# Moving the two parts of the normed input to a pool of their own, at the front of the on-chip memory

## The chip, the cores and the metric

The kernel runs on one core of a Trainium2 chip. The metric is the device time of one execution in microseconds (us); of several runs the median is given.

## The reference, cut to what matters

One layer of a model with four parallel mixers. The input `x` (512 rows of 1024) is normed and multiplied by one wide weight matrix; the columns of the product are the inputs of the four mixers and the gates:

```
h = rms_norm(x, norm_g)                      # 512 x 1024
proj = h @ w_in                              # 1024 x 11208, split into 19 parts
y_a = chunked_spatial_gating(a_u, a_v, ...) * silu(a_z)
y_b = dsa_attention(b_q, b_c, ...)          * silu(b_z)   # top 128 keys of each query
y_c = short_gated_conv(c_b, c_c, c_x, ...)  * silu(c_z)
y_d = forgetting_attention(d_q, d_k, d_v, d_f, ...) * silu(d_z)
branch = einsum('nbsw,nwd->bsnd', [y_a, y_b, y_c, y_d], w_branch)
merged = sum(sigmoid(gates) * branch, axis=n)
out = rms_norm(x + merged @ w_out, final_g)
```

## The kernel before, in words

**Numbers in two parts.** All large products run in float32r on TensorE. To keep float32's precision each operand is split into a high part (rounded to float32r by ScalarE) and a low part (the rest, a subtraction on VectorE or GpSimd); a product is then the sum of three matmuls, high by high, high by low, low by high. The helper is `split` (lines 73 to 81; its instructions appear as L76, L77, L79 and L80).

**The normed input** lies on chip in its two parts, `hh` and `hl`, from start to end. Each has 128 partitions of 8 x 512 float32r numbers (16,384 bytes in each partition): feature within a block of 128 along the partitions, then the block `k` (0 to 7), then the 512 rows of `x`. They are written once, by `transposed_x` (L230 to L237), and read by every product with `w_in`:

- `proj_fm` (L110 to L121) is called 80 times. Each call makes 24 matmuls into one PSUM tile `ps_fm`: the weights `wh`, `wl` are the stationary operand (128 x 128), and a whole row block of `hh` or `hl` is the moving operand (512 columns).
- `term_tm` (L139 to L142) makes three matmuls with the input as the stationary operand and 512 columns of weights moving. It is used with `hh`, `hl` for `ps_dv` (L246 to L250, 96 matmuls) and for `ps_va` (L594 to L598, 96 matmuls), and with the merged branches `mh`, `ml` for `ps_o` at the end (L791 to L795).

```
114	        for k in range(NK):
115	            nc.tensor.matmul(ps[:m], wh[:, k, :], hh[:, k, :], start=(k == 0), stop=False)
116	            nc.tensor.matmul(ps[:m], wh[:, k, :], hl[:, k, :], start=False, stop=False)
...
119	        for k in range(NK):
120	            nc.tensor.matmul(ps[:m], wl[:, k, :], hh[:, k, :], start=False, stop=(k == NK - 1))
...
140	        nc.tensor.matmul(ps, ah, wh, start=(k == 0), stop=False)
```

(The first argument is the output, the second the stationary, the third the moving operand.)

**Order of the work.** First the input is normed and transposed, with the products for the attention's values between (`ps_dv`). Then come the small projections of the sparse attention and its scores (`dots`, L456 and L457), the values of the first mixer (`ps_va`), and the search for the top 128 keys: 16 rounds of max and match-replace on VectorE (L471 and L472), handed out step by step between projections by `point()`. Both attentions run in the same way between projections (`lg` logits, `pt_ps` transposes, `po` values). From about 303 us on, four pairs of `gated` (L716) and `merge` (L733) follow: a merge computes a gate by `proj_fm`, and after each gate the branch product `pb` of the one before (L742, L743 and L745, 12 matmuls each, with `yh`, `yl` moving). In each merge the last branch product follows directly on the one before it. Last comes the output product `ps_o`. Instructions are placed by a scheduler that keeps each engine's order fixed in the finished program.

**Where tiles lie.** A pool's tiles are laid one behind the other in the order of their allocation, each rounded up to 32 bytes in a partition, and pools are laid in the order in which they are opened: `const`, `wpool`, `sb`. In the program the first pool begins at byte 16,512 of each partition (258 x 64). `const` begins with these:

```
ident  512 bytes   at 16512  (258 x 64)
negh    32         at 17024  (266 x 64)
causal 512         at 17056  (266 x 64 + 32)
up    2048         at 17568  (274 x 64 + 32)
hh   16384         at 19616  (306 x 64 + 32)
hl   16384         at 36000  (562 x 64 + 32)
bfB     16         at 52384  (818 x 64 + 32)
prm    180         at 52416  (819 x 64), and from here on multiples of 64
```

All tiles of `wpool` (weights and raw weights) and all larger tiles of `sb` (among them `yh`, `yl`, `mh`, `ml`) begin at multiples of 64 bytes, and so do the slices of them that the 128 x 128 and 512-column operands named above read.

Of the kernel before, what the change touches and what calls it, by code (L numbers as in the profile page):

```python
# [9 lines left out]
F32R = mybir.dt.float32r  # L10
# [7 lines left out]
P = 128  # L18
S = 512
# [3 lines left out]
NK = D // P  # L23
# [10 lines left out]
def hybrid_kernel(ctx: ExitStack, tc, x, norm_g, w_in, gm_ln_g, gm_ln_b, gm_w_s, gm_b_s,  # L34
# [2 lines left out]
    x, w_in, out = x[0], w_in[0], out[0]  # L37
    PSUM = bass.MemoryType.PSUM

    const = ctx.enter_context(tc.tile_pool(name="const", bufs=1))  # L40
    wpool = ctx.enter_context(tc.tile_pool(name="wpool", bufs=1))
    sb = ctx.enter_context(tc.tile_pool(name="sb", bufs=1))
# [168 lines left out]
                            pattern=[[1, S]], channel_multiplier=-1)  # L211
    nc.vector.tensor_copy(up, upf)

    hh = const.tile([P, NK, S], F32R, name="hh")
    hl = const.tile([P, NK, S], F32R, name="hl")

    def norm_x(t):
        xt = xts[t // 2][:, t % 2, :]
# [649 lines left out]
```

## Time and profile before

| | |
|---|---|
| median of 3 runs | 718.44 us (717.96 to 719.29) |
| profiled execution, its own time | 719.16 us |
| span in its profile | 717.5 us, granted TensorE clock 0.999 |
| TensorE matmuls | 3139, busy 703.9 us of the span |
| VectorE, ScalarE, GpSimd busy | 361.3, 276.1, 170.6 us |

The span is the time from the first to the last instruction on the core; the rest of an execution's own time, 1.7 us here, lies around it. Matmuls are pipelined: the duration given for one reaches past the start of the next. So the pace of TensorE is read not from durations but from the distance between the starts of successive matmuls. In a timeline, successive instructions of one kind are merged into a row ("x8"), whose start is that of the first. In the view by stretches, an instruction that runs over a border is counted on both sides.

### The profile page before, as it was taken

What the parts mean: (1) busy time and instruction counts of PE and PEld (TensorE: products, weight loads), DVE (VectorE), ACT (ScalarE), POOL (GpSimd) and SP (SyncE); (2) the same over time, 40 slices, a digit from 0 to 9 for tenths busy, and PEclk for the clock granted to TensorE, in tenths of its full rate; (3) what the DMA queues carried; (4) which work ended last, traced back from release to release, by engine and by line L of the source; (5) the groups of instructions that cost most, each with busy time, mean ns of one, the idle gap of its engine ahead of it and who ended that gap; (6) DMA issues with size and microseconds to landing.
All of it is one profiled execution on the core that took longest, in us unless ns stands there. A gap on an engine that the chain in (4) does not pass through costs nothing.

```text
span 717.5 us, 8000 instructions
## 1 busy us (share of the span) xinstructions
PE 703.9 (98%) x3139; PEld 564.8 (79%) x3139; DVE 361.3 (50%) x638; ACT 276.1 (38%) x439; POOL 170.6 (24%) x110
## 2 busy tenths in 40 slices
PE   7999999998999999999999999999999999999996
PEld 4878767787888888888888888888888888888885
DVE  5725699999763755534222442233422334333454
ACT  4616354345545656333232232222322223333232
POOL 1000487342232422112000121113211131111101
PEclk9999999999999999999999999999999999999999
DMA  6715031322121122223133131331313313133133
GB/s 235 220 60 153 3 117 59 103 75 60 58 89 59 60 63 94 79 88 118 60 117 112 64 118 60 117 118 58 118 59 117 118 58 118 59 117 118 59 118 117
DMA packets 56817, 68.05 MB, mean 95 GB/s; under 512 B 3582, under 2 KB 45067, under 8 KB 56780
## 3 DMA queue, kind: packets, MB, share of 16 engines
q1 hardware_dynamic: 55900, 65.46, 27.9%
q0 software_dynamic: 304, 1.05, 0.5%
q10 hardware_dynamic: 576, 1.05, 0.4%
q8 instruction: 24, 0.39, 0.2%
q14 instruction: 13, 0.11, 0.0%
HBM read 64.80 MB, written 2.10 MB: 93 GB/s over the span
## 4 chain that ended last, share of the span: by engine, by line
PE 90%; DVE 6%; DMA 2%; issue 1%; ACT 0%; SPq 0%; POOLq 0%; POOL 0%
PE ps_fm L115 20%; PE ps_fm L116 20%; PE ps_fm L120 19%; PE pb L742 4%; PE pb L743 4%; PE pb L745 4%; DVE sc L472 2%; PE ps_o L142 2%; PE ps_o L141 2%; PE ps_o L140 2%; DVE m L471 2%; PE ps_va L141 1%; PE pt_ps L531 1%; PE ps_va L140 1%; PE ps_dv L140 1%; PE ps_va L142 1%
## 5 line engine op out<-in xcount | busy, mean ns | idle before, releaser
L115 PE MATMUL ps_fm<-hh,wh 128*128 128x512 f32 (+1 forms) x640 | 254.1, 397 | 0.0
L116 PE MATMUL ps_fm<-hl,wh 128*128 128x512 f32 (+1 forms) x640 | 253.5, 396 | 0.0
L120 PE MATMUL ps_fm<-hh,wl 128*128 128x512 f32 (+1 forms) x640 | 166.2, 396 | 0.0
L115 PEld LDWEIGHTS ps_fm<-hh,wh 128*128 128x128 f32 (+1 forms) x640 | 119.7, 187 | 29.2 <-issue 0.9
L116 PEld LDWEIGHTS ps_fm<-hl,wh 128*128 128x128 f32 (+1 forms) x640 | 119.7, 187 | 28.4 <-issue 0.2
L120 PEld LDWEIGHTS ps_fm<-hh,wl 128*128 128x128 f32 (+1 forms) x640 | 118.9, 187 | 28.6 <-issue 0.2
L76 ACT ACTIVATE wh<-raw 128x1024 fp32r<-128x1024 f32 x78 | 82.4, 1058 | 117.5 <-PE ps_fm L116 87.4
L77 DVE TENSOR_TENSOR wl<-raw,wh 128x1024 fp32r<-128x1024 f32 x50 | 61.0, 1222 | 83.3 <-PE ps_fm L120 71.4
L77 POOL TENSOR_TENSOR wl<-raw,wh 128x1024 fp32r<-128x1024 f32 x28 | 69.3, 2481 | 108.4 <-PE ps_fm L120 46.6
L751 POOL TENSOR_TENSOR acc<-acc,sg 128x512 f32<-128x512 f32 x24 | 41.7, 1738 | 160.6 <-DVE sg L750 160.6
L742 PE MATMUL pb<-yh,wh 128*128 128x512 f32 x128 | 50.4, 393 | 0.0
L743 PE MATMUL pb<-yl,wh 128*128 128x512 f32 x128 | 50.1, 392 | 0.0
L77 DVE TENSOR_TENSOR wl<-rawb,wh 128x1024 fp32r<-128x1024 f32 x16 | 19.6, 1226 | 53.9 <-PE ps_fm L120 38.7
L76 ACT ACTIVATE wh<-rawb 128x1024 fp32r<-128x1024 f32 x16 | 17.0, 1060 | 52.2 <-PE ps_fm L116 52.2
L750 DVE TENSOR_TENSOR sg<-pb,sg 128x512 f32<-128x512 f32 x24 | 16.6, 692 | 37.1 <-PE pb L745 37.1
L745 PE MATMUL pb<-yh,wl 128*128 128x512 f32 x128 | 34.2, 389 | 0.0
L769 ACT ACTIVATE sg<-ps_fm 128x512 f32<-128x512 f32 x32 | 19.1, 598 | 26.3 <-PE ps_fm L120 26.3
L742 PEld LDWEIGHTS pb<-yh,wh 128*128 128x128 f32 x128 | 24.0, 188 | 5.7
L743 PEld LDWEIGHTS pb<-yl,wh 128*128 128x128 f32 x128 | 24.0, 188 | 5.6
L745 PEld LDWEIGHTS pb<-yh,wl 128*128 128x128 f32 x128 | 24.0, 188 | 5.1
L517 ACT ACTIVATE l<-l,nm 128x128 f32<-128x128 f32 (+3 forms) x32 | 17.9, 560 | 23.2 <-DVE nm L515 23.1
L725 POOL TENSOR_TENSOR sg<-sg,oa 128x512 f32<-128x512 f32 x4 | 6.9, 1719 | 82.3 <-ACT sg L724 78.5
(242 smaller groups left out, 927.8 us busy)
## 6 DMA issues: line engine op xcount, KB each, us to landing
raw<-in_w_in_dram SPq DMA_DIRECT2D x39, 1024.0 KB, 4.9
rawb<-in_w_branch_dram SPq DMA_DIRECT2D x8, 1024.0 KB, 5.0
rawt<-in_w_out_dram SPq DMA_DIRECT2D x4, 1024.0 KB, 4.9
xt<-in_x_dram SPq DMA_DIRECT2D x4, 512.0 KB, 7.3
rawt<-in_w_in_dram SPq DMA_DIRECT2D x4, 512.0 KB, 7.5
rawt<-in_w_in_dram SPq DMA_DIRECT2D x2, 1024.0 KB, 5.5
xr<-in_x_dram SPq DMA_DIRECT2D x2, 1024.0 KB, 4.9
out_dram<-o SPq DMA_DIRECT2D x4, 256.0 KB, 2.1
```

Of the source, the lines that this page charges most:

```text
L76: nc.scalar.activation(hi, src, AF.Copy)
L77: eng.tensor_tensor(lo, src, hi.bitcast(F32), op=ALU.subtract)
L115: nc.tensor.matmul(ps[:m], wh[:, k, :], hh[:, k, :], start=(k == 0), stop=False)
L116: nc.tensor.matmul(ps[:m], wh[:, k, :], hl[:, k, :], start=False, stop=False)
L120: nc.tensor.matmul(ps[:m], wl[:, k, :], hh[:, k, :], start=False, stop=(k == NK - 1))
L140: nc.tensor.matmul(ps, ah, wh, start=(k == 0), stop=False)
L141: nc.tensor.matmul(ps, ah, wl, start=False, stop=False)
L142: nc.tensor.matmul(ps, al, wh, start=False, stop=(k == NK - 1))
L742: nc.tensor.matmul(pb, bh[:, k, cs_], yh[:, k, :], start=(k == 0), stop=False)
L743: nc.tensor.matmul(pb, bh[:, k, cs_], yl[:, k, :], start=False, stop=False)
L745: nc.tensor.matmul(pb, bl[:, k, cs_], yh[:, k, :], start=False, stop=(k == NH - 1))
L751: nc.gpsimd.tensor_tensor(acc, acc, sg, op=ALU.add)
```

## The change

A pool `act` is opened ahead of `const`, and `hh` and `hl` are allocated in it at once, not in `const` behind `up`. Nothing else is touched; every instruction reads and writes the same tiles.

```
@@ -37,6 +37,10 @@
     x, w_in, out = x[0], w_in[0], out[0]
     PSUM = bass.MemoryType.PSUM
 
+
+    act = ctx.enter_context(tc.tile_pool(name="act", bufs=1))
+    hh = act.tile([P, NK, S], F32R, name="hh")
+    hl = act.tile([P, NK, S], F32R, name="hl")
     const = ctx.enter_context(tc.tile_pool(name="const", bufs=1))
     wpool = ctx.enter_context(tc.tile_pool(name="wpool", bufs=1))
     sb = ctx.enter_context(tc.tile_pool(name="sb", bufs=1))
@@ -211,8 +215,6 @@
                             pattern=[[1, S]], channel_multiplier=-1)
     nc.vector.tensor_copy(up, upf)
 
-    hh = const.tile([P, NK, S], F32R, name="hh")
-    hl = const.tile([P, NK, S], F32R, name="hl")
 
     def norm_x(t):
         xt = xts[t // 2][:, t % 2, :]
```

By the rule of the layout, `hh` moves from byte 19,616 to 16,512 and `hl` from 36,000 to 32,896 (258 x 64 and 514 x 64). `ident`, `negh`, `causal` and `up` move up by 32,768 bytes and keep their remainders by 64. From `bfB` on, every tile stays where it was.

## Rows read from the trace of the kernel before

**Rows 1.** The page: busy time of the engines, and the chain that ended last

```profile
PE 703.9 (98%) x3139; PEld 564.8 (79%) x3139; DVE 361.3 (50%) x638; ACT 276.1 (38%) x439; POOL 170.6 (24%) x110
...
PE 90%; DVE 6%; DMA 2%; issue 1%; ACT 0%; SPq 0%; POOLq 0%; POOL 0%
```

**Rows 2.** Busy time by stretch: stretch, length, then busy (count) of PE, PEld, DVE, ACT, POOL

```profile
65.00:95.00 30.00, 30.00 (x135) 22.49 (x134) 19.78 (x33) 14.20 (x26) 15.75 (x13) 1.00 0.15 45
95.00:127.75 32.75, 32.75 (x127) 23.03 (x127) 32.51 (x66) 14.22 (x21) 24.12 (x13) 1.00 0.30 97
127.75:168.50 40.75, 39.03 (x179) 30.82 (x177) 40.75 (x117) 19.57 (x38) 14.41 (x6) 1.00 0.24 78
168.50:303.00 134.50, 134.19 (x671) 112.14 (x672) 83.53 (x194) 70.93 (x147) 40.36 (x20) 1.00 0.23 75
303.00:667.00 364.00, 364.00 (x1572) 293.94 (x1571) 127.21 (x136) 112.22 (x137) 67.29 (x40) 1.00 0.29 94
```

**Rows 3.** Timeline of TensorE, one `proj_fm` (24 matmuls) and the next one's start

```profile
505.51 0.39 PE L115 MATMUL ps_fm<-hh,wh 128*128 128x512 f32 x1
505.74 0.40 PE L116 MATMUL ps_fm<-hl,wh 128*128 128x512 f32 x1
...
509.25 2.03 PE L120 MATMUL ps_fm<-hh,wl 128*128 128x512 f32 x8
511.11 0.39 PE L115 MATMUL ps_fm<-hh,wh 128*128 128x512 f32 x1
```

**Rows 4.** Timeline of TensorE, `ps_va`: first and last of 31 matmuls in a row

```profile
68.55 0.40 PE L140 MATMUL ps_va<-wh,hh 128*128 128x512 f32 x1
...
75.55 0.40 PE L140 MATMUL ps_va<-wh,hh 128*128 128x512 f32 x1
```

**Rows 5.** Timeline of TensorE, `ps_o`: first and last of 100 matmuls in a row

```profile
667.19 0.39 PE L140 MATMUL ps_o<-wh,mh 128*128 128x512 f32 x1
...
689.63 0.39 PE L140 MATMUL ps_o<-wh,mh 128*128 128x512 f32 x1
```

**Rows 6.** Timeline of TensorE, the last two branch products of the last merge

```profile
661.71 0.40 PE L742 MATMUL pb<-yh,wh 128*128 128x512 f32 x1
...
663.56 1.07 PE L745 MATMUL pb<-yh,wl 128*128 128x512 f32 x4
664.47 0.39 PE L742 MATMUL pb<-yh,wh 128*128 128x512 f32 x1
```

**Rows 7.** Matmuls of `ps_fm` by stretch: stretch, length, busy (count)

```profile
0.00:45.00 45.00, 4.00 (x16) 1.00 0.63 205
45.00:95.00 50.00, 19.26 (x82) 1.00 0.19 56
95.00:168.50 73.50, 59.50 (x240) 1.00 0.27 86
168.50:303.00 134.50, 104.13 (x409) 1.00 0.23 75
303.00:667.00 364.00, 279.23 (x1177) 1.00 0.29 94
```

**Rows 8.** The same of `ps_dv` (first two rows) and of `ps_va` (the last)

```profile
0.00:19.63 19.63, 5.34 (x12) 1.00 0.67 231
19.63:45.00 25.37, 20.83 (x85) 1.00 0.60 185
...
45.00:95.00 50.00, 23.90 (x96) 1.00 0.19 56
```

**Rows 9.** Timeline of TensorE, two of the first `ps_dv` matmuls

```profile
13.05 0.63 PE L142 MATMUL ps_dv<-dvwh,hl 128*128 128x512 f32 x1
13.48 0.63 PE L140 MATMUL ps_dv<-dvwh,hh 128*128 128x512 f32 x1
```

**Rows 10.** Timeline of TensorE, 163 to 170 us: the rows with idle time before them

```profile
166.03 0.50 PE L85 MATMUL po<-ptl,vfh 128*128 128x512 f32 x1 [1.38 <-DVE ptl L77]
...
168.81 0.44 PE L531 MATMUL pt_ps<-ident,l 128*128 128x128 f32 x2 [0.66 <-ACT l L520]
```

More of the change, by code (lines that the diff above doesn't have):

```diff
@@ L38, in hybrid_kernel @@
     PSUM = bass.MemoryType.PSUM
+    act = ctx.enter_context(tc.tile_pool(name="act", bufs=1))
+    hh = act.tile([P, NK, S], F32R, name="hh")
+    hl = act.tile([P, NK, S], F32R, name="hl")
     const = ctx.enter_context(tc.tile_pool(name="const", bufs=1))
@@ L212, in hybrid_kernel @@
     nc.vector.tensor_copy(up, upf)
-    hh = const.tile([P, NK, S], F32R, name="hh")
-    hl = const.tile([P, NK, S], F32R, name="hl")
     def norm_x(t):
```

## Prediction, made before the change was run

> **What bounds the kernel.** I read the page first: TensorE is busy 98% of the span and 90% of the chain that ended last is TensorE's own work; VectorE, the next, is busy 50% and has 6% of the chain [rows 1]. By stretches, TensorE is busy without a gap from 65 to 127.75 us and from 303 to 667 us, and nearly so from 168.5 to 303 (134.19 of 134.50 us); only from 127.75 to 168.5 is another engine full too: VectorE, 40.75 of 40.75 us, where the top-128 search runs, and already 32.51 of 32.75 us in the stretch before [rows 2]. So, outside some 70 us around the search, what one matmul costs is what the kernel costs, and there are about 3,000 of them.
>
> A matmul's duration doesn't tell its cost, since the next starts before it ends. I therefore divided distances between starts in the timeline by the number of matmuls. A `proj_fm` of 24 goes from 505.51 to 511.11 us: 5.60/24 = **233.3 ns** each [rows 3]. The output product, of the same width, goes from 667.19 to 689.63 us with 99 steps: 22.44/99 = **226.7 ns** [rows 5]. The second of two branch products in a row takes 664.47 to 667.19 us for 12: also 226.7 ns [rows 5, 6]. And `ps_va` needs 7.00/30 = 233.3 ns [rows 4].
>
> The pair that tells most is `ps_va` and `ps_o`: the same three lines of code, the same shapes, moving operands from the same pool of weights. They differ in the stationary operand: `hh`, `hl` in the slow one, `mh`, `ml` in the fast one. In `proj_fm` `hh` and `hl` move and the weights stand, and the pace is the slow one again. So the 6.6 ns go with `hh` and `hl`, in either role. What sets these two apart from the other operands in the listing of the layout is their start: 32 bytes past a multiple of 64, where all the others start at a multiple. The size fits a reading in blocks of 64 bytes: a row of 512 numbers (2,048 bytes) lies in 32 blocks if it starts at a border and touches 33 if not, and a 32nd of 226.7 ns is 7.1 ns, near the 6.6 measured. That is an inference, not a row; but other engines' work is no candidate, since the slow pace holds where VectorE is full (65 to 168 us) and where it is a third busy (303 to 667) [rows 2, 3, 4].
>
> **The change, part by part.** No instruction is added or removed, and no wait or transfer moves in the program. `hh` and `hl` come to start at multiples of 64 (16,512 and 32,896), so each of their slices does; `ident`, `negh`, `causal` and `up` keep their remainders, all other tiles their places. I cost these other edits at nothing: the same bytes are read and written by the same instructions.
>
> The price per matmul that reads `hh` or `hl` is then 233.3 - 226.7 = 6.6 ns. By stretch:
>
> 1. Up to 19.63 us: 12 products of `ps_dv`, 0.43 us apart [rows 8, 9]. At that pace something else holds them; saving 0.
> 2. 19.63 to 95 us: 85 of `ps_dv`, 96 of `ps_va` [rows 8], 16 + 82 of `ps_fm` [rows 7], together 279 x 6.6 ns = 1.84 us. VectorE is not full here (19.78 of 30 us from 65 to 95 [rows 2]), so its later work starts earlier by as much.
> 3. 95 to 168.5 us: 240 of `ps_fm` [rows 7], 1.58 us on TensorE. VectorE is full throughout and TensorE waits at the end of it, 1.38 us for VectorE and 0.66 us for ScalarE, which is fed by VectorE [rows 10]. A quicker TensorE comes sooner to that wait and waits longer. I take 0; the bounds are 0 and 1.58 us.
> 4. 168.5 to 303 us: 409 x 6.6 ns = 2.70 us [rows 7]. TensorE leaves 0.31 us idle and VectorE is busy 83.53 of 134.50 us [rows 2]. I take all of it; if the second attention's steps through VectorE and ScalarE were to hold TensorE, it would be down to 0.
> 5. 303 to 667 us: 1177 x 6.6 ns = 7.77 us [rows 7]. VectorE, ScalarE and GpSimd are busy 127, 112 and 67 of 364 us [rows 2], so nothing is there to take the bound over.
> 6. Branch products after a projection: the first eight matmuls take 661.71 to 663.56 us, 231.3 ns each, before the pace falls to 226.7 [rows 6], as if the slow pace lingered. If it does so because of `hh` and `hl`, it goes: 8 x 4.6 ns = 0.037 us, in 7 of the 8 products of each of 4 merges (the last follows another branch product): 28 x 0.037 = 1.03 us. I take it; the lower bound is 0. The short attention products between projections may have a like tail; at most 0.3 us, not counted.
> 7. 667 us to the end: `ps_o` is at 226.7 ns already; 0.
>
> Sum: 1.84 + 2.70 + 7.77 + 1.03 = 13.3 us. The profiled execution took 719.16 us by its own time, 717.5 of it span; it is 0.7 us above the median of 718.44. It should become 705.9, and the median 718.44 - 13.3 = **705.1 us**, 1.9% less. With the upper bound of step 3 and the 0.3 us of step 6 it is 703.2; with the tails kept and step 4 lost, 708.8.
>
> **A rule that speaks against it.** The rows show 6.6 ns between operands that start 32 bytes apart from a multiple of 64 and those that start at one [rows 4, 5]. The Trainium skill, page "SBUF — State Buffer", section "Specifications (TRN2)", says that this memory is read in lines of 16 bytes and that each step to a new line has its price. By that, a start at byte 19,616 (1,226 x 16) is at a line's start as much as 16,512 (1,032 x 16), and the sum would be 0, not 13.3 us. The section "Operand start alignment" of the same page calls a start at any multiple of the element's size legal, and says that nothing was timed there. Its lines alone leave the 6.6 ns unexplained, so I go by the rows.
>
> **The rivals.**
>
> *No effect.* The 6.6 ns belong to something else that `hh` and `hl` share: their place in the low part of the memory, which hardly changes, or the long step between their blocks, while a start 32 bytes on costs nothing; or the pool doesn't come to lie where I worked it out. For it: no row shows these two operands at another start. Against it: the two paces are each exact over dozens of matmuls [rows 3, 4, 5], and the difference is near a 32nd. The time stays **718.4 us**. (The Trainium skill's lines of 16 bytes, "SBUF — State Buffer", "Specifications (TRN2)", would lead here.)
>
> *Given back around the attentions.* Steps 2, 3 and 4 yield nothing, since from the search to 303 us the steps of the softmax through VectorE and ScalarE decide. For it: VectorE is full for 70 us [rows 2], TensorE waits for it [rows 10]. Against it: 0.31 us of idle TensorE in the 134 us after. Left are 7.77 + 1.03 = 8.8 us: **709.6 us**.
>
> *Slower.* With `hh` and the weights both starting at a border, the two reads of a matmul and of the weight load under it meet at the same borders each time and one waits for the other, by one block each: +6.6 ns in place of -6.6, in the 1,865 matmuls of steps 2, 4 and 5: +12.3 us, **730.7 us**. It decides as soon as the pace of `ps_fm` between 303 and 667 us is above 233.3 ns. Against it: in `ps_o` and the late `pb` both operands start at a border, and they are the fast ones [rows 5, 6].
>
> **How the numbers follow.** Forecast 0.83; given back 0.06; no effect 0.08; slower 0.03. The range reaches from 703.0 (the upper bounds of steps 3 and 6) to 710.0 us (past the second rival); it leaves out the other two, 0.11, and the rest is for unknown costs. A measurement of this kernel can tell about 0.2%, 1.4 us, from no change. Faster by more: 0.83 + 0.06 = 0.89; within it 0.08; slower 0.03.
>
> **What would show it.** In the profile after, a `proj_fm` between 303 and 667 us should span 24 x 226.7 = 5.44 us, `ps_va` 226.7 ns a step, the mean duration of a `ps_fm` matmul should come down to that of `ps_o`, and `pb` after a projection should be at 226.7 ns from its first matmul. Step 3 is right if TensorE's waits around 164 to 169 us grow by about 1.6 us. `ps_o` should stay as it is. The prediction is wrong at its root if `ps_fm` keeps 233.3 ns; it is wrong in steps 2 to 4 alone if the pace falls everywhere but the branch stages begin less than 4.5 us earlier than 303 us.

## The result and the profile after

The changed kernel takes **710.61 us** (median of 4 runs, 708.76 to 711.89) beside 718.80 us of the kernel before in the same rounds: a ratio of 0.9885 [0.9859, 0.9911], 8.2 us less. The forecast was 705.1 us, 13.3 us less; the result lies 0.6 us above the range. The profiled execution took 711.89 us, 710.2 of it span.

The page of the changed kernel answers rows 1. TensorE is busy 10 us less, and VectorE's share of the chain that ended last has gone from 6% to 11%:

```profile
PE 693.9 (98%) x3139; PEld 566.4 (80%) x3139; DVE 364.5 (51%) x638; ACT 275.1 (39%) x439; POOL 169.9 (24%) x110
...
PE 85%; DVE 11%; DMA 2%; issue 1%; ACT 0%; SPq 0%; POOLq 0%; POOL 0%; DVEq 0%
```

The pace came out as forecast. One `proj_fm` in the timeline of TensorE (rows 3 before) goes from 496.69 to 502.13 us, 5.44 us for 24 matmuls, 226.7 ns each in place of 233.3:

```profile
496.69 0.39 PE L119 MATMUL ps_fm<-hh,wh 128*128 128x512 f32 x1
...
500.32 1.98 PE L124 MATMUL ps_fm<-hh,wl 128*128 128x512 f32 x8
502.13 0.39 PE L119 MATMUL ps_fm<-hh,wh 128*128 128x512 f32 x1
```

`ps_va` (rows 4 before) needs 68.00 to 74.81 us for 30 steps, 227.0 ns each. The last two branch products (rows 6 before) start 2.72 us apart, and the output product 2.72 us after them: 12 x 226.7 ns from the first matmul on, so the slow tail behind a projection is gone.

```profile
654.45 0.39 PE L744 MATMUL pb<-yh,wh 128*128 128x512 f32 x1
...
657.17 0.39 PE L744 MATMUL pb<-yh,wh 128*128 128x512 f32 x1
...
659.89 0.39 PE L144 MATMUL ps_o<-wh,mh 128*128 128x512 f32 x1
```

What went wrong stands in the view by stretches (rows 2 before; columns as there). From 127.75 to 168.5 us TensorE is busy 36.20 of 40.75 us, where it had 39.03, and the counts show it behind: 160 matmuls in place of 179.

```profile
65.00:95.00 30.00, 30.00 (x137) 22.83 (x136) 19.47 (x33) 14.66 (x26) 16.43 (x14) 1.00 0.15 44
95.00:127.75 32.75, 32.75 (x129) 23.09 (x128) 32.61 (x69) 14.23 (x21) 22.91 (x12) 1.00 0.35 114
127.75:168.50 40.75, 36.20 (x160) 27.75 (x159) 40.75 (x107) 16.86 (x34) 12.75 (x6) 1.00 0.20 64
...
168.50:303.00 134.50, 134.31 (x676) 114.17 (x677) 86.45 (x200) 71.84 (x151) 41.84 (x21) 0.99 0.22 69
303.00:667.00 364.00, 364.00 (x1611) 301.70 (x1610) 131.41 (x140) 113.82 (x141) 69.44 (x41) 1.00 0.30 99
```

The order of the instructions on each engine is the same in both programs, so the n-th matmul of one trace can be set against the n-th of the other. Its start is earlier after the change by 1.22 us at 95 us, 1.72 at 127.75 and 1.90 at 140; then it is **later** by 2.85 us at 168.5 and by 1.63 at 303; at 667 it is earlier by 7.29. So the change gained until 140 us, lost some 4.8 us in the next 28, and gained again. In the view of waits (engine, tile and line, what it waited for: us in total, times, longest), TensorE has more of them in the attention, all on VectorE or on ScalarE behind it; before there were two, `po` on `ptl` with 1.38 and `pt_ps` on `l` with 0.66 us [rows 10]:

```profile
PE nb_ps L440 <- DVE rl L84: 1.5, 1, 1.5
PE po L89 <- DVE ptl L81: 1.5, 1, 1.5
PE pt_ps L533 <- DVE l L515: 0.9, 1, 0.9
PE pt_ps L533 <- ACT l L522: 0.7, 2, 0.4
```

**What held VectorE.** Its instructions are the same ones in the same order. From 95 to 168.5 us one kind takes longer: the addition of the causal mask in the forget-gate attention, `l += causal` (L509 before, L511 after), 128 columns, both inputs in on-chip memory. There are 16; one takes 0.26 to 0.30 us as a rule. The timelines of VectorE and of GpSimd before, the additions and the GpSimd splits `wl` beside them:

```profile
137.09 0.47 DVE L509 TENSOR_TENSOR l<-l,causal 128x128 f32<-128x128 f32 x2
...
145.73 2.14 DVE L509 TENSOR_TENSOR l<-l,causal 128x128 f32<-128x128 f32 x1
...
156.81 0.26 DVE L509 TENSOR_TENSOR l<-l,causal 128x128 f32<-128x128 f32 x1
...
137.65 2.41 POOL L77 TENSOR_TENSOR wl<-raw,wh 128x1024 fp32r<-128x1024 f32 x1 [4.69 <-PE ps_fm L120]
145.32 2.40 POOL L77 TENSOR_TENSOR wl<-raw,wh 128x1024 fp32r<-128x1024 f32 x1 [5.27 <-ACT wh L76]
...
157.20 2.40 POOL L77 TENSOR_TENSOR wl<-raw,wh 128x1024 fp32r<-128x1024 f32 x1 [2.15 <-ACT pth L76]
```

The additions at 137.09 and 156.81 are over just before a split begins: 137.09 + 0.47 = 137.56 against 137.65, and 157.07 against 157.20. The one at 145.73 begins inside a split, takes 2.14 us and ends 0.15 us after it. After the change the first two stand like this:

```profile
135.89 2.67 DVE L511 TENSOR_TENSOR l<-l,causal 128x128 f32<-128x128 f32 x2
...
157.76 1.97 DVE L511 TENSOR_TENSOR l<-l,causal 128x128 f32<-128x128 f32 x1
...
135.82 2.40 POOL L81 TENSOR_TENSOR wl<-raw,wh 128x1024 fp32r<-128x1024 f32 x1 [4.61 <-PE ps_fm L124]
...
157.20 2.39 POOL L81 TENSOR_TENSOR wl<-raw,wh 128x1024 fp32r<-128x1024 f32 x1 [1.20 <-ACT pth L80]
```

The split waits for a matmul (`<-PE ps_fm`) and so comes 1.83 us earlier (135.82 for 137.65); the addition waits its turn on VectorE, which had gained only 1.20 us (135.89 for 137.09). The split is now first, by 0.07 us, and the addition lasts until it is over: the first of the two took 2.47 us (the longest of its group of 16, whose median is 0.277) and ended at 138.36, 0.14 us after the split's end at 138.22. The second case ends alike: 157.76 + 1.97 = 159.73, the split's end 159.59. Here the split stands at 157.20 in both traces; it is the addition that comes 0.95 us later than before, since the first hold-up had set VectorE back. Without the hold-up these two would have cost 0.26 us each, so 2.2 + 1.7 = 3.9 us are lost on an engine that has no idle time from 127.75 to 168.5 us. (The addition at 145.73 us, 146.73 after the change, was held in both, 2.14 and 2.09 us.) The Trainium skill, page "SBUF — State Buffer", section "SBUF: two separate sides", says that VectorE and GpSimd share a pair of ports under an exclusive lock, held for a whole instruction, which a VectorE instruction with two inputs in this memory needs and which the loser waits out. These rows agree, to 0.14 us.

**The clock.** Behind these waits, in which TensorE was busy 1.61 of 3.00 us (165 to 168) and 0.31 of 1.00 (168 to 169), its granted clock (third column from the right) fell from 2.4 to 1.2 GHz, half, and came back at 173 us. The profile before has no such fall there.

```profile
168.50:170.00 1.50, 1.31 (x5) 1.22 (x6) 1.50 (x4) 0.98 (x3) 1.50 (x1) 0.81 0.00 0
170.00:171.00 1.00, 1.00 (x6) 1.00 (x6) 1.00 (x4) 0.39 (x3) 0.07 (x1) 0.50 0.02 8
171.00:172.00 1.00, 1.00 (x8) 1.00 (x7) 1.00 (x4) 1.00 (x3) 0.00 (x0) 0.50 0.71 181
172.00:173.00 1.00, 1.00 (x5) 0.85 (x4) 1.00 (x5) 0.73 (x3) 0.00 (x0) 0.57 1.09 386
173.00:174.00 1.00, 1.00 (x6) 0.82 (x5) 1.00 (x4) 0.31 (x1) 0.00 (x0) 1.00 1.07 377
```

The starts of the same two matmuls before (first two lines) and after the change show what came when:

```profile
166.36 0.39 PE L86 MATMUL po<-pth,vfl 128*128 128x512 f32 x1
...
169.56 0.39 PE L115 MATMUL ps_fm<-hh,wh 128*128 128x512 f32 x1
...
169.03 0.40 PE L90 MATMUL po<-pth,vfl 128*128 128x512 f32 x1
...
172.92 0.40 PE L119 MATMUL ps_fm<-hh,wh 128*128 128x512 f32 x1
```

At 169.03 us, before the clock fell (0.81 from 168.5 to 170 us puts the fall near 169.4), TensorE was already 2.67 us behind, where it had been 1.90 ahead at 140. Over the half clock it fell back by 0.69 us more. In that piece the kernel before waited 0.66 us [rows 10], so of the 5.3 us lost since 140 between 0.7 and 1.4 are the clock's; the rest are the late steps of VectorE.

Two questions were left for runs: is the hold-up the cause of the missing 5 us, or is VectorE simply full; and is the start of `hh` and `hl` at a multiple of 64 what makes the pace?

### The profile page after: what moved, and what is told of

Same layout as the page of the kernel before. It is cut to its first block, busy times and chain, and to the rows that moved or that the text cites. A ratio compares the mean times of both kernels' runs of the same rounds, so it can differ in the third digit from the quotient of the medians.

```text
span 710.2 us, 8000 instructions
## 1 busy us (share of the span) xinstructions
PE 693.9 (98%) x3139; PEld 566.4 (80%) x3139; DVE 364.5 (51%) x638; ACT 275.1 (39%) x439; POOL 169.9 (24%) x110
## 4 chain that ended last, share of the span: by engine, by line
PE 85%; DVE 11%; DMA 2%; issue 1%; ACT 0%; SPq 0%; POOLq 0%; POOL 0%; DVEq 0%
PE ps_fm L119 18%; PE ps_fm L120 18%; PE ps_fm L124 18%; PE pb L744 4%; PE pb L745 4%; PE pb L747 4%; DVE sc L474 3%; DVE m L473 2%; PE ps_o L144 2%; PE ps_o L146 2%; PE ps_o L145 2%; DVE sc L466 1%; PE pt_ps L533 1%; PE ps_dv L144 1%; DVE l L511 1%
## 5 line engine op out<-in xcount | busy, mean ns | idle before, releaser
L119 PE MATMUL ps_fm<-hh,wh 128*128 128x512 f32 (+1 forms) x640 | 251.3, 393 | 0.0
L120 PE MATMUL ps_fm<-hl,wh 128*128 128x512 f32 (+1 forms) x640 | 250.0, 391 | 0.0
L124 PE MATMUL ps_fm<-hh,wl 128*128 128x512 f32 (+1 forms) x640 | 162.5, 391 | 0.0
L145 PE MATMUL ps_o<-wl,mh 128*128 128x512 f32 (+1 forms) x72 | 26.2, 366 | 0.0
```

The costliest lines, as they stand in the source:

```text
L145: nc.tensor.matmul(ps, ah, wl, start=False, stop=False)
```

## Experiments 1: where the missing 5 us went

**The mask by TensorE.** In both kernels the VectorE addition is replaced by one more matmul of 128 columns per logits tile (for it the mask and the identity are also copied to float32r, not shown).

```
             if fox:
+                nc.tensor.matmul(ps[:, qs], ident_r, causal_r, start=False, stop=True)
...
-                nc.vector.tensor_tensor(l[:, qs], l[:, qs], causal, op=ALU.add)
```

> The changed kernel, with the forget-gate attention's addition of the causal mask (VectorE, two inputs in SBUF, 16 of them, 0.26 us each where nothing disturbs them, 1.97 to 2.67 us three times in the changed kernel's profile) replaced by one more TensorE matmul of 128 columns for each logits tile, which adds the mask into the logits' PSUM tile. Theory (the gain was given back because a GpSimd split held two more of these additions up, 2.2 and 1.7 us, on a VectorE that has no room between 95 and 168 us, and the clock then fell): no such addition, no hold-up, TensorE's waits at 161 to 169 us (0.85, 0.45, 1.48 us) nearly gone, no fall of the clock at 169 us: 710.6 - 3.9 - 1.0 (clock) + 1.0 (16 matmuls of some 0.06 us) = 706.7 or, if the third addition and the 16 times 0.26 us count too, down to 703. Rival A (VectorE is full there whatever holds it up, so that TensorE's gain in this stretch can't reach the end): 709 to 711. Rival B (the fall of the clock alone took the gain and comes with any timing): 709 to 712, with half a clock again for some microseconds after the attention.

> The kernel before with the same replacement (mask added by TensorE); the two parts of the normed input stay at 32 bytes past a multiple of 64. Theory: one held-up addition (1.9 us) and 1.38 + 0.66 us of TensorE's waits go, 1.0 us of matmuls comes: 716.5 to 718; against the changed kernel with the same replacement the difference is the whole sum of the prediction, 13 us (12 to 14.5). Rivals A and B: the difference stays at the 8 us that was measured.

Measured: **705.17 us** (705.12 to 705.82, 5 runs) for the changed kernel with it, ratio to the kernel before 0.9813 [0.9800, 0.9826]; 718.41 us (717.70 to 719.17) for the kernel before with it, ratio 0.9992 [0.9983, 1.0001]. Their difference is 13.2 us; the prediction's sum was 13.3. (718.41 lies just above the 716.5 to 718 expected.) In the changed one TensorE waits once from 115 to 310 us, 0.3 us at 120, and the granted clock is 1.00 throughout the attention. Both rivals had asked for 8. But this edit also takes 16 times 0.26 us of work off VectorE, which leaves the rival "VectorE is full" half alive.

**The changed kernel again**, as the base line of that chip:

> The changed kernel as it is, as the base line of this chip: 708.8 to 711.9 by every theory; two or three held-up mask additions between 135 and 160 us in its profile.

712.02 us (711.32 to 713.33), 0.1 above what was expected and 7.0 below the kernel before in the same rounds; three held additions (2.41, 2.09 and 1.96 us), TensorE's 1.5 us wait for `ptl` again, and the clock at 0.85 and 0.81 between 165 and 175 us.

**The same addition with one input elsewhere.** VectorE adds the mask as before, 16 times, but into the logits in PSUM ahead of their eviction, so that one input lies in PSUM, TensorE's output memory, and one in the on-chip memory where both lay before.

```
             if fox:
+                nc.vector.tensor_tensor(ps[:, qs], ps[:, qs], causal, op=ALU.add)
                 nc.vector.scalar_tensor_tensor(l[:, :n], ps[:, :n], cq[:, i, h:h + 1],
...
-                nc.vector.tensor_tensor(l[:, qs], l[:, qs], causal, op=ALU.add)
```

> The changed kernel, with the forget-gate attention's mask added on VectorE as before (16 additions of 128 columns), but into the logits' PSUM tile ahead of the eviction: one operand in PSUM and one in SBUF in place of two in SBUF. VectorE keeps the number of its instructions; TensorE gets nothing more. Theory (what costs the time is that an addition with both operands in SBUF is held until a GpSimd split ends): none of the 16 takes over 0.5 us, TensorE's waits at 161 to 169 us go, no fall of the clock there: 704 to 707, as the kernel with the mask on TensorE (705.17). Rival (VectorE's load counts, and the kernel with the mask on TensorE gained because it took 16 times 0.26 us off it): 709 to 712, TensorE's waits in 161 to 169 us stay at 2 us or more.

> The kernel before with the same replacement. Theory: 716.5 to 719, and 12 to 14.5 us above the changed kernel with it. Rival: 717 to 720, some 8 us above it.

Measured: **705.57 us** (704.56 to 706.10), ratio 0.9817 [0.9802, 0.9832], for the changed kernel; 717.45 us (717.09 to 719.73), ratio 0.9990 [0.9980, 1.0000], for the one before: 11.9 us apart, just under the 12 to 14.5 expected. The group of the 16 additions in the changed one (duration min/median/max in ns), and two of them beside GpSimd splits that had already begun:

```profile
L509 DVE TENSOR_TENSOR lg<-lg,causal x16: 268/278/300, 131.4 to 204.8; 128x128 f32<-128x128 f32 x16
...
136.06 0.27 DVE L509 TENSOR_TENSOR lg<-lg,causal 128x128 f32<-128x128 f32 x1
...
163.15 0.28 DVE L509 TENSOR_TENSOR lg<-lg,causal 128x128 f32<-128x128 f32 x1
...
134.90 2.40 POOL L81 TENSOR_TENSOR wl<-raw,wh 128x1024 fp32r<-128x1024 f32 x1 [4.60 <-PE ps_fm L124]
...
163.13 2.40 POOL L81 TENSOR_TENSOR wl<-raw,wh 128x1024 fp32r<-128x1024 f32 x1 [5.64 <-ACT wh L80]
```

They run in the middle of a split (136.06 lies in 134.90 to 137.30) and take 0.27 us. VectorE's load is that of the changed kernel (a median of 278 ns for 277), it is still full (40.75 of 40.75 us), TensorE waits once from 100 to 310 us, 0.9 us, and the changed kernel is 13.0 us below the kernel before in the same rounds, where it had been 8.2. The kernel before gains 1.1 us itself by the edit, its own held addition gone, so the pair is 11.9 us apart; with the mask by TensorE it was 13.2. That settles the first question: not the load of VectorE but the hold-up, and with it the late steps of the attention and the fall of the clock, took them.

The two changed kernels without the hold-up are also the fastest of the study, at least 5 us below the change alone and 13 below the kernel before.

## Experiments 2: what sets the 6.6 ns

Four kernels were meant to change the start of the parts alone. Two keep the remainder of 32 or make it 16 and 48 in the new pool, two put the parts at a multiple of 64 in the old pool or at another multiple in the new one.

```
pad32:    act.tile([P, 8], F32, name="pad0")       # one ahead of hh, one behind hl; 8 numbers = 32 bytes
off16:    hh_t = act.tile([P, NK * S + 8], F32R, name="hh")
          hl_t = act.tile([P, NK * S + 8], F32R, name="hl")
          hh, hl = (a[:, 4:4 + NK * S].rearrange("p (k s) -> p k s", s=S) for a in (hh_t, hl_t))
inplace:  const.tile([P, 8], F32, name="pad0")     # kernel before; one ahead of hh, one behind hl
pad64:    act.tile([P, 16], F32, name="pad0")      # ahead of hh
```

> As the changed kernel, but with 32 unused bytes ahead of hh and 32 behind hl: hh and hl stay in their pool at the front and start 32 bytes past a multiple of 64 again. Theory (the start decides): steady steps of ps_fm and ps_va 233.3 ns, one slow x + causal addition on VectorE as in the kernel before, time 718 to 720 us. Rival (the place at the front, or the pool of their own, decides): 226.7 ns and 709 to 712 us.

> The kernel before, hh and hl left in const behind up, with 32 unused bytes ahead of hh and 32 behind hl, so that only their start moves, to a multiple of 64. Theory (the start decides): 226.7 ns a step, the same three slow additions of causal on VectorE as in the changed kernel, time 709 to 712 us. Rival (the place decides): 233.3 ns and 718 to 720 us.

> As the changed kernel, but hh starts 16 and hl 48 bytes past a multiple of 64 (a border of 16 bytes, not of 64). Theory (blocks of 64 bytes are read, and a block more costs 6.6 ns whatever the offset): 233.3 ns a step, 718 to 720 us. Rival (lines of 16 bytes, or a start that has to be a multiple of 16): 226.7 ns a step and 709 to 712 us. Third way (the cost grows with the offset): hh and hl steps differ from each other.

> As the changed kernel, with 64 unused bytes ahead of hh: hh and hl start at odd multiples of 64, where all the other operands start at multiples of 128. Theory (blocks of 64 bytes): 226.7 ns a step, 709 to 712 us. Rival (blocks of 128 bytes): 233 ns or more, 718 us or more.

Measured: pad32 718.75 us (ratio 0.9999 [0.9990, 1.0008]), off16 718.97 (1.0006 [0.9997, 1.0015]), inplace 710.87 (0.9895 [0.9865, 0.9925]), pad64 709.21 (one run). So neither the pool nor the order matters, and all four fit blocks of 64 bytes. That reading did not last.

The traces of inplace and pad64 also price the clock. Both show the first hold-up (2.40 and 2.45 us) and the one that the kernel before has too, but not the second of the changed kernel, which was expected for inplace. There the clock fell earlier, at 150 us, some 1.1 us after a wait of TensorE of 1.5 us (the changed kernel has that wait too, 1.49 us, without a fall). At 150 us the matmuls of inplace are 0.07 us ahead of those of the kernel before, at 155 they are 1.42 behind. TensorE is busy without a gap between, at a mean clock of 0.66, which is 3.4 us at half, so these 3.4 us cost 1.5:

```profile
149.36 0.50 PE L440 MATMUL nb_ps<-rl,up 4*128 4x512 f32 x1 [1.50 <-DVE rl L80]
...
150.00:155.00 5.00, 5.00 (x18) 4.05 (x18) 5.00 (x17) 3.92 (x8) 1.59 (x1) 0.66 0.00 0
```

So which waits and which fall of the clock follow differs from kernel to kernel, at nearly the same time in the end; what they share is the first hold-up.

**One part off the border.** 32 bytes between the parts (and 32 behind `hl`), or ahead of both and between them:

```
lowonly32:   hh = act.tile(...); act.tile([P, 8], F32, name="pad0"); hl = act.tile(...); act.tile([P, 8], ...)
highonly32:  act.tile([P, 8], F32, name="pad0"); hh = act.tile(...); act.tile([P, 8], ...); hl = act.tile(...)
```

> The changed kernel with 32 bytes between the two parts: the high part at a multiple of 64 bytes, the low part 32 past one. Theory (a matmul pays some 6.6 ns where its own operand begins off a multiple of 64): in a projection two of three matmuls read the high part, so the mean of ps_fm is 226.7 + 6.6/3 = 228.9 ns in place of 226.7 or 233.3, and ps_va and ps_dv likewise; the time is some 13/3 = 4.4 us above the undisturbed gain: 709 to 715, and at most as fast as the changed kernel. Rival (the pair of parts counts as one, or the pool does it): 226.7 or 233.3 throughout, and 710 or 718.

> The changed kernel with 32 bytes ahead of the high part and none ahead of the low part's border: the high part 32 past a multiple of 64 bytes, the low part at one; two of three matmuls of a projection read the misplaced part, where the kernel with the low part alone misplaced (ps_fm 233.0 ns) had one of three. If each matmul paid for its own operand, and the misplaced low part had cost more than its share for a reason of its own: 231.1 ns. If one misplaced operand among three costs as much as three (the rows so far): 232.5 to 233.5 ns and 717 to 719.

Measured: lowonly32 718.24 us (717.01 to 719.12), ratio 0.9989 [0.9980, 0.9999]; highonly32 715.60 (one run). In the timelines, the distance of two successive rows of eight low-weight matmuls is one set of 24; lowonly32 first, then highonly32:

```profile
503.28 2.02 PE L126 MATMUL ps_fm<-hh,wl 128*128 128x512 f32 x8
...
508.86 2.03 PE L126 MATMUL ps_fm<-hh,wl 128*128 128x512 f32 x8
```

```profile
501.02 2.02 PE L126 MATMUL ps_fm<-hh,wl 128*128 128x512 f32 x8
...
506.58 2.02 PE L126 MATMUL ps_fm<-hh,wl 128*128 128x512 f32 x8
```

5.58 and 5.56 us. By the border, lowonly32 with one misplaced part in three matmuls should need 5.49 (24 x 228.9 ns), and even its eight matmuls in a row that read `hh` alone, at a multiple of 64, take 508.86 + 1.87 = 510.73 to the next row: 233.8 ns each. The border fails here. What these two and the four before them had also changed: every tile behind the pads, the weights among them, had moved by 64 bytes.

**The weights moved, the parts kept.** A pad behind `hl` alone (64 or 32 bytes):

```
     hl = act.tile([P, NK, S], F32R, name="hl")
+    act.tile([P, 16], F32, name="pad0")        # padw32: 8
```

> The changed kernel with 64 bytes behind the low part, so that both parts stay where they are (0 past a multiple of 128 bytes) and every tile after them, the projections' weights among them, moves by 64. If the border of 64 bytes under each operand decides (the prediction's rule): ps_fm 226.7 ns, 709 to 712. Rival (the place of the parts against the weights decides: in the three fast kernels so far parts and weights begin at the same place within 128 bytes, in all slow ones they don't): 231 to 234 ns, 715 to 719.

> The changed kernel with 32 bytes behind the low part: both parts at a multiple of 64 bytes, all weights 32 past one. If the border of the streamed operand alone decides: 226.7 ns in ps_fm, where the parts are streamed. If either operand off the border lengthens the whole run of matmuls (as one part of two off it did): 231 to 234 ns in ps_fm and ps_va, and 715 to 719; pb, whose operands are weights and tiles that move along, 226.7 to 234.

Measured: 718.26 and 718.30 us, one run each, beside 718.20 of the kernel before, also one. Both have the parts exactly where the change puts them. padw64:

```profile
502.95 2.03 PE L125 MATMUL ps_fm<-hh,wl 128*128 128x512 f32 x8
...
508.55 2.03 PE L125 MATMUL ps_fm<-hh,wl 128*128 128x512 f32 x8
```

5.60 us a set, the pace of before, with every operand at a multiple of 64. The rival of that run holds: the place of the parts **against the weights** decides.

**The counter-test and the period.** The kernel before with 32 bytes behind `hl` (parts left off the border, weights brought level with them), and the change with two or four small tiles of 64 bytes moved ahead of the parts, the weights left where they are:

```
beforew32:   hl = const.tile([P, NK, S], F32R, name="hl"); const.tile([P, 8], F32, name="pad0")
shift128:    early = [act.tile([P, 16], F32, name="ls%d" % i) for i in range(2)]   # ahead of hh; shift256: 4
```

> The kernel before with 32 bytes behind the low part and nothing else: both parts stay at 32 bytes past a multiple of 64, as before, and every tile of the pools after them, the weights among them, moves by 32, so that parts and weights start at the same place within 512 bytes. If the place against the weights decides: ps_fm 226.7 ns, and a time like the changed kernel's, 708.5 to 713.5. If a border of 64 bytes under each operand decides: now both operands are off it, 233.3 ns or more, 717 to 722.

> The changed kernel with two small tiles of 64 bytes moved from the end of their pool to ahead of the parts: the parts begin 128 bytes later against the weights, all three at multiples of 128. If the place against the weights decides and counts within 128 bytes: 226.7 ns and 708.5 to 713.5. If it counts within more: 231 to 234 ns, 715 to 719.

> The same with four such tiles: 256 bytes against the weights. Within 128 or 256 bytes: 226.7 ns, 708.5 to 713.5; within 512: 231 to 234 ns, 715 to 719.

Measured: beforew32 **710.51 us** (709.26 to 711.85), ratio 0.9876 [0.9858, 0.9895], from one line in the kernel before; shift128 717.19 and shift256 710.10 (one run each). Sets of 24 in beforew32, shift128 and shift256:

```profile
499.75 1.98 PE L120 MATMUL ps_fm<-hh,wl 128*128 128x512 f32 x8
...
505.19 1.98 PE L120 MATMUL ps_fm<-hh,wl 128*128 128x512 f32 x8
```

```profile
501.97 2.03 PE L125 MATMUL ps_fm<-hh,wl 128*128 128x512 f32 x8
...
507.57 2.03 PE L125 MATMUL ps_fm<-hh,wl 128*128 128x512 f32 x8
```

```profile
503.86 1.98 PE L125 MATMUL ps_fm<-hh,wl 128*128 128x512 f32 x8
...
509.30 1.98 PE L125 MATMUL ps_fm<-hh,wl 128*128 128x512 f32 x8
```

5.44, 5.60 and 5.44 us. All thirteen kernels of this question, with the starts by the rule of the layout (the first weight tile is at byte 78,464 before and after; all weight tiles lie a multiple of 4,096 apart):

| kernel | `hh`, `hl` past a multiple of 64 | weights minus `hh`, `hl`, remainder by 256 | one set of 24, us |
|---|---|---|---|
| before | 32, 32 | 224, 224 | 5.60 |
| pad32 | 32, 32 | 32, 32 | 5.61 |
| off16 | 16, 48 | 48, 16 | 5.61 |
| padw32 | 0, 0 | 32, 32 | 5.60 |
| padw64 | 0, 0 | 64, 64 | 5.60 |
| shift128 | 0, 0 | 128, 128 | 5.60 |
| lowonly32 | 0, 32 | 64, 32 | 5.58 |
| highonly32 | 32, 0 | 32, 0 | 5.56 |
| after, inplace, pad64, shift256 | 0, 0 | 0, 0 | 5.44 |
| beforew32 | 32, 32 | 0, 0 | 5.44 |

The second column doesn't sort the last; the third does. A row of matmuls has the quick pace where streamed operand and weights begin at the same remainder by 256 ("level" from here on); in every kernel where they don't, 16 to 224 bytes off, it hasn't. What a mixture costs is open: in highonly32 one matmul in three is level, and (226.7 + 2 x 233.3)/3 = 231.1 ns would make 5.55 us a set for 5.56 measured, but its `ps_va`, with the same mixture, goes from 68.06 to 75.06 us in 30 steps, 233.3 ns each, as if none were.

Why it is so is not shown. The next weights are loaded beside the running matmul (PEld is busy 79% of the span [rows 1]), so the two reads run side by side, and that they get into each other's way unless they are in step would fit. That is a guess: no run took the weight load away.

## Why the prediction was right and wrong

The gain of each stretch, as the difference of the starts of the same matmul in two traces at the stretch's ends, for the change and for the two pairs without the hold-up:

| step | predicted | before to after | pair, mask in PSUM | pair, mask by TensorE |
|---|---|---|---|---|
| 1 and 2, to 95 us | 1.84 | 1.22 | 2.03 | 1.19 |
| 3, 95 to 168.5 | 0 (0 to 1.58) | **-4.07** | 1.00 | 0.65 |
| 4, 168.5 to 303 | 2.70 | 1.22 | 1.85 | 1.94 |
| 5 and 6, 303 to 667 | 8.80 | 8.92 | 8.87 | 8.91 |
| 7, to the end | 0 | -0.03 | 0.03 | -0.05 |
| sum | 13.3 | 7.3 | 13.8 | 12.6 |

The sums are those of single profiled executions. The two pairs stand 11.9 and 13.2 us apart by their medians; most of what their two columns differ by lies in the first 20 us, and from there on they give 12.7 and 12.6.

- **Step 3 failed**, in its bounds: "A quicker TensorE comes sooner to that wait and waits longer. I take 0; the bounds are 0 and 1.58 us." It excluded a loss; the stretch lost 4.07 us. VectorE's work was taken as fixed in length, with TensorE waiting at its end. But a GpSimd split, released by TensorE, came 1.83 us earlier and VectorE's own queue only 1.20, so that one addition, and through the delay a second, fell behind a split: 3.9 us on a full engine, and the fall of the clock behind it. The prediction's own sign for a fault in steps 2 to 4, a branch stage that begins less than 4.5 us earlier, came: it begins 1.63 us later. The price stood in the trace of before: the one held addition at 145.73 us took 2.14 us where its 15 fellows take some 0.27. With 16 such additions and a split of 2.4 us every 5 to 8 us, one or two more hold-ups were a bound to set, 2 to 4 us of loss. With the hold-up out of the way the stretch gives 1.00 and 0.65 us, inside the bounds as they stood.
- **Steps 5 and 6** hold to some 0.1 us, and `pb` lost its slow tail as forecast. **Step 2** is within 0.7 us in all pairs; the first 20 us alone differ by up to 1.1 us between two traces.
- **Step 4** was some 0.8 us too large even without the hold-up (1.85 and 1.94 for 2.70), since 6.6 ns for each matmul was too much there. In the pair with the mask in PSUM the 372 steps from one projection matmul to the next gain 1.62 us in this stretch, 4.4 ns each, where from 303 to 667 us they gain 6.7: behind the attention's short products the changed kernel's projection matmuls start 227 to 232 ns apart and settle at 226.7 only after some ten, while the kernel before is at 231 to 234 from the second on. Why the pace lingers is not shown. With the change alone 0.6 us less arrives; the clock is back at full only at 173 us, inside this stretch.
- **The sum's price was right and its reason wrong.** "What sets these two apart [...] is their start: 32 bytes past a multiple of 64" is true of the layout, but the 33rd block is not what costs: padw64 has none and is slow, beforew32 has them and is quick. The change works by luck: `hh`, at 16,512, happens to lie 242 x 256 bytes ahead of the weights, and nobody had set that. The multiple of 64 that was aimed at gave nothing. The rows offered the other reading as well: `ps_o` and `pb`, the quick ones, read operands that, by the rule of the layout, are all level with the weights. One reading of the rows was also wrong: VectorE was called full from 65 to 168 us, but it is busy 19.78 of 30 us from 65 to 95 [rows 2], where `ps_va` stands. Nothing in the sum hung on it.
- **The rivals.** "No effect" and "slower" are out by the pace; the latter had the sign reversed, since operands that are level are the quick ones. "Given back around the attentions" named the right stretch and, at 709.6 us, nearly the time, but by other terms; its mechanism, that the softmax's steps through VectorE decide, fell with the mask in PSUM, which leaves VectorE its load and brings the gain.
- **The rule on lines of 16 bytes**, weighed in the prediction (the Trainium skill, "SBUF — State Buffer", "Specifications (TRN2)"), gave no effect. A start off a multiple of 64 indeed costs nothing by itself (beforew32). The same page says, in "SBUF: two separate sides", that TensorE never waits on anyone, and lists a second, independent port for the weight load under "A bandwidth-pool intuition that's wrong (but worth ruling out)". By that one would not expect the place of one operand against the other to matter. It does, by 6.6 ns of 233.3 here, and the rows decide.

## What to carry to other kernels

Where a long row of matmuls loads new weights each time, bring the start of the streamed operand level with the start of the weights, by 256 bytes, before looking at any border; a pad of 32 bytes was worth 8 us here (beforew32). Where an engine is full, what another engine does to the length of its instructions is part of the bound: look in the trace for the few long ones among many alike, and for what ran beside them. Here it was a VectorE addition with two inputs in on-chip memory beside a GpSimd split of 2.4 us; with one input in PSUM none of the 16 took more than 0.30 us.

## What was not expected of the hardware

- In a row, matmuls of 512 float32r columns start every 226.7 ns where streamed and loaded operand are level by 256 bytes and every 232.5 to 233.8 where none is, whatever their own remainders by 64 (5.44 against 5.58 to 5.61 us a set, table above).
- With the parts in the loaded role the loss is not the same at every distance: 30 steps of `ps_va` take 6.81 us after the change (227.0 ns each), 6.87 in padw64 (64 bytes off, 229.0), 6.97 in shift128 (128 off, 232.3) and 7.00 in padw32 (32 off, 233.3).
- A matmul pace 2.8% quicker made the kernel slower in one stretch by 4.07 us, through an order of 0.07 us between two other engines: a VectorE addition of 0.27 us then took 2.47.
- 3.4 us at half clock cost a TensorE that is busy throughout 1.5 us (inplace).
